# Low weights first, a written-out order, and another address for the values in a two-layer attention trunk

## The chip, the cores and the metric

The kernel runs on one core of a Trainium2 chip. The metric is the device time of one execution in microseconds (us). TensorE (PE) multiplies and adds up in PSUM; ScalarE (ACT), VectorE (DVE) and GpSimd (POOL) do the elementwise work; SyncE (SP) issues the loads. In the profile, PEld is the loading of a product's stationary operand.

## The reference

Two layers, 256 tokens of 1024 channels, everything in float32. A layer normalises its input once, projects it with one matrix of 9808 columns, and splits the result into queries, keys, values and gates of three attention branches (a, b, c) of 8 heads of 64, the small indexer of branch b, the forget logits of branch c and the merge gates:

```python
h = rms_norm(x, gain)
proj = jnp.einsum('bsd,de->bse', h, w_in)
...
y = jnp.einsum('nbsw,nwd->bsnd', jnp.stack([oa, ob, oc], axis=0), w_branch)
gates = jax.nn.sigmoid(merge_logit).reshape(B, S, N_BRANCH, D_MODEL)
merged = jnp.sum(gates * y, axis=2)
return x + jnp.einsum('bsd,de->bse', merged, w_out)
```

Branch a is causal attention, branch b attends to the 64 best keys of its indexer, branch c adds a decay to its logits. Each branch's output is multiplied by its SiLU gate. A final normalisation ends the trunk.

## The kernel before

**Products in halves.** Every float32 operand of a large product is split into a high half, rounded to the matmul's format (tiles `wh`, `hTh`, `og0h`), and a low half, the rest (`wl`, `hTl`, `og0l`). A product is then three: high by high, high weights by the low half of the input, low weights by the high half of the input. ACT makes the high half of a piece of weights (L450), DVE the low half (L454), from a raw tile that SP has loaded; there are six buffers for each half.

**Units.** `unit_b` computes 128 columns of the projection for all 256 tokens: eight steps along the channels, 24 products of 256 columns, cut into four groups of six that the order treats as one operation each (`mm_ops`, L492). Weights are the stationary operand, the normalised input `hTh`/`hTl` moves. `UNIT_ORDER` says how high (nh) and low (nl) products follow each other; the first group holds six high products and no low one. There are 64 such units in a layer: four of the indexer (qi), twelve of each branch (queries q, keys k, gates g, of four pairs of heads), and 24 merge gates (m00 to m27: branch, then block of 128 channels). `unit_y` is the product with the branch matrix, 12 products in two groups; `unit_a` multiplies the other way around, with the input stationary and 512 columns of weights moving, for values (va, vb; L1119 in the first layer, and L1179 in `va_units`) and for the output matrix (o00, o01, o10, o11: half of the columns, then half of the tokens). Units write to one of three PSUM banks (`proj`).

**Attention.** For each pair of heads: scores (`qk`, L713 and L715) into two banks `s`; row minimum and bias on DVE (L781), exponentials on ACT (L785), rounding into a high and a low half (L793 on ACT or L796 on DVE, L800 on DVE), a transpose by DMA for each head (L809, from `e` to `t`), copies of the transposed weights to `pt` (L814 on ACT or L815 on DVE), the product with the values (`av`, L827 to L830) into the one bank `o`. ACT (L843) and DVE (L845) empty that bank into `ot`, L848 applies the gate, and L482/L483 split the result. Evacuations of units: L992 (merge gates, ACT), L1023 and L1025 (branch products, DVE), L742 (gates), L541 to L544 (rotary embedding), L858 to L872 (keys).

**The value tiles.** `V` is two tiles of 8192 bytes per partition. They hold the high and low halves of the values, and are the stationary operand of `av`. At the end of a layer they hold the merged branches and are the stationary operand of the output products (names `proj<-wh,v`). The two tiles stand behind `ncs` and `csum`, 64 bytes each, and begin at 128 modulo 512 bytes.

**The order.** All work after the start is given to a planner as numbered operations (3226 of them, numbered in the order in which the program makes them), each with its engines, its cost, its dependencies, its buffers and a key. The planner walks through modelled time: for each engine it takes, among the operations that can start within `SLACK` of the earliest, the one with the lowest key. `SHIFT` moves keys of single operations by hand, and `WAY` shifts the choice between ACT and DVE (or POOL and DVE) for those that can run on either. The instructions are emitted in that order, so that each engine has a fixed queue; at run time, semaphores alone decide when each starts. PE, ACT, DVE and POOL work their queues strictly in that order, and SP issues weight loads, row loads and transposes in one queue.

**The numbers that the prediction names.** On PE: 1285 is the second `av` of branch b in layer 0, 2578 and 2623 are the two of the second half of branch c in layer 1; 1500 and 1515 are the first groups of the merge gate units m13 and m15 of layer 0. On ACT: 1236 and 1238 empty the bank after the first `av` of branch b, 1270 is the first copy of transposed weights for 1285 and 1284 the last, 1323 writes half of a query tile, 1361 a key tile, 1491 and 1498 are high halves of merge gate weights. On DVE: 1499 is the low half for m13, 3069 and 3076 are those for m14 and m15 of layer 1, 3181 multiplies the first half of the last 128 rows by the final gain. On SP: 1269 and 1282 are the transposes for 1285.

Of the kernel before, what the change touches and what calls it, by code (L numbers as in the profile page):

```python
# [38 lines left out]
STEP = 24.0  # L39
# [5 lines left out]
SLACK = {"PE": 0.0, "ACT": 110.0, "DVE": 110.0, "SP": 1500.0}  # L45
# [12 lines left out]
UNIT_ORDER = ((6, 1), (3, 1), (3, 2), (2, 1), (1, 2), (1, 1))  # L58
# [5 lines left out]
def constants(forget_bias):  # L64
# [26 lines left out]
SHIFT = {  # L91
# [1217 lines left out]
```

## Time and profile before

| | |
|---|---|
| runs | 597.23, 594.69, 596.69 us; median 596.69 |
| profiled execution | 597.11 us, span 595.3 us, granted clock 0.999 |
| TensorE busy | 585.3 us, 98% of the span, 4704 products |
| VectorE, ScalarE, GpSimd busy | 537.7 us, 464.6 us, 94.7 us |
| read from memory | 103.42 MB, 175 GB/s over the span |

A row of groups gives line, engine, operation, output and inputs by the program's names (buffer numbers left out), shapes and count, then busy time in us and mean ns of one, then the engine's idle time just before them and what ended it. A row of the timeline gives start in us, duration in us, and the instruction; equal neighbours are merged (`x2`), and idle time before it stands in brackets. A row of the chain gives start, duration and what the time went to. Products are pipelined: a product's duration reaches into the next ones, so the pace is the distance between starts.

### The profile page before, as it was taken

How to read it: one execution, taken by the hardware profiler on the slowest of the kernel's cores; microseconds unless marked ns; L12 is line 12 of the kernel's file. 1: busy time of each engine (PE TensorE's matmuls, PEld its weight loads, DVE VectorE, ACT ScalarE, POOL GpSimd, SP SyncE). 2: the span in 40 equal slices, each digit the busy share in tenths (PEclk: the TensorE clock that was granted, in tenths of full speed). 3: DMA queues.
4: the chain of work that ended last, by engine and by line, in shares of the span. 5: the costliest groups of instructions: out<-in, count | busy, mean ns of one | idle time of the engine just before them, and what ended most of it. 6: DMA issues, size and time to landing. Idle time of an engine off the chain costs nothing.

```text
span 595.3 us, 12660 instructions
## 1 busy us (share of the span) xinstructions
PE 585.3 (98%) x4704; PEld 566.8 (95%) x4704; DVE 537.7 (90%) x1357; ACT 464.6 (78%) x1006; POOL 94.7 (16%) x103
## 2 busy tenths in 40 slices
PE   8999999999999998999999999999999999999996
PEld 7999999999998998999889999999999989999985
DVE  8879999999899988999685999999999989999883
ACT  6669579997998778975585776899889876999741
POOL 1034041100000224200000510430100004330100
PEclk9999999999999999999999999999999999999999
DMA  8994485798867758296747547697869686655911
GB/s 307 300 300 142 142 264 118 223 219 260 200 188 169 237 179 183 72 267 229 227 142 248 177 143 216 178 225 167 245 184 279 129 222 192 183 141 119 325 36 72
DMA packets 136511, 116.83 MB, mean 196 GB/s; under 512 B 42753, under 2 KB 127361, under 8 KB 136449
## 3 DMA queue, kind: packets, MB, share of 16 engines
q1 hardware_dynamic: 136160, 115.59, 67.5%
q8 instruction: 37, 0.61, 0.4%
q10 hardware_dynamic: 288, 0.43, 0.2%
q14 instruction: 26, 0.20, 0.1%
HBM read 103.42 MB, written 1.05 MB: 175 GB/s over the span
## 4 chain that ended last, share of the span: by engine, by line
PE 89%; DVE 3%; DMA 3%; ACT 3%; issue 1%; POOL 0%; SPq 0%; POOLq 0%; DVEq 0%; ACTq 0%
PE proj L492 75%; PE proj L1179 4%; DMA t<-e 2%; PE s L715 2%; PE proj L1119 2%; PE s L713 2%; PE o L827 1%; PE o L830 1%; DMA raw<-in_x_dram 1%; DVE wl L454 1%; ACT e L785 1%; ACT wh L450 1%; PE o L829 0%; PE o L828 0%; DVE e L800 0%
## 5 line engine op out<-in xcount | busy, mean ns | idle before, releaser
L492 PE MATMUL proj<-hTl,wh 128*128 128x256 f32 x1024 | 264.1, 276 | 0.0
L492 PE MATMUL proj<-hTh,wh 128*128 128x256 f32 x1024 | 263.9, 277 | 0.2 <-DVE mth L1023 0.2
L454 DVE TENSOR_TENSOR wl<-raw,wh 128x1024 fp32r<-128x1024 f32 x180 | 220.4, 1235 | 13.1 <-ACT wh L450 12.0
L492 PE MATMUL proj<-hTh,wl 128*128 128x256 f32 x1024 | 226.2, 277 | 0.0
L450 ACT ACTIVATE wh<-raw 128x1024 fp32r<-128x1024 f32 x180 | 188.3, 1055 | 43.4 <-PE proj L492 34.6
L492 PEld LDWEIGHTS proj<-hTh,wh 128*128 128x128 f32 x1024 | 192.2, 188 | 0.6 <-issue 0.4
L492 PEld LDWEIGHTS proj<-hTl,wh 128*128 128x128 f32 x1024 | 192.2, 188 | 0.1
L492 PEld LDWEIGHTS proj<-hTh,wl 128*128 128x128 f32 x1024 | 172.1, 188 | 0.0
L542 POOL TENSOR_TENSOR rsh<-rsh,cst 128x256 f32<-128x256 f32 x40 | 35.6, 891 | 342.4 <-DVE rsh L541 324.1
L544 POOL TENSOR_TENSOR rr<-rr,rsh 128x256 f32<-128x256 f32 x40 | 44.1, 1103 | 3.1
L785 ACT ACTIVATE e<-e,st 128x128 f32<-128x128 f32 (+1 forms) x96 | 42.6, 445 | 2.0 <-DVE st L781 1.7
L800 DVE SCALAR_TENSOR_TENSOR e<-e,st 128x128 f16<-128x128 f32 (+1 forms) x96 | 39.8, 425 | 0.9 <-ACT e L793 0.4
L814 ACT ACTIVATE pt<-t 128x384 fp32r<-128x384 f16 x73 | 34.3, 514 | 7.4 <-DMA t<-e 6.0
L492 PE MATMUL proj<-wh,v 128*128 128x512 f32 (+1 forms) x144 | 35.2, 366 | 0.0
L492 PE MATMUL proj<-og0l,wh 128*128 128x256 f32 x128 | 33.9, 277 | 0.0
L793 ACT ACTIVATE e<-e,st 128x256 f16<-128x256 f32 (+1 forms) x77 | 32.0, 444 | 0.8 <-DVE e L800 0.2
L492 PE MATMUL proj<-og0h,wh 128*128 128x256 f32 x128 | 32.5, 277 | 0.0
L492 PEld LDWEIGHTS proj<-wh,v 128*128 128x128 f32 x144 | 25.3, 189 | 4.2
L492 PE MATMUL proj<-og0h,wl 128*128 128x256 f32 x128 | 28.8, 278 | 0.0
L492 PEld LDWEIGHTS proj<-og0h,wh 128*128 128x128 f32 x128 | 24.1, 188 | 0.0
L492 PEld LDWEIGHTS proj<-og0l,wh 128*128 128x128 f32 x128 | 24.1, 188 | 0.0
L845 DVE TENSOR_TENSOR ot<-o,ot 64x256 f32<-64x256 f32 x48 | 19.9, 414 | 3.5 <-ACT ot L843 2.7
(225 smaller groups left out, 1072.3 us busy)
## 6 DMA issues: line engine op xcount, KB each, us to landing
raw<-in_w_in_dram SPq DMA_DIRECT2D x74, 1024.0 KB, 5.6
raw<-in_w_branch_dram SPq DMA_DIRECT2D x24, 512.0 KB, 4.1
raw<-in_w_out_dram SPq DMA_DIRECT2D x8, 1024.0 KB, 7.9
raw<-in_x_dram SPq DMA_DIRECT2D x8, 256.0 KB, 5.8
tmp<-wf SPq DMA_DIRECT2D x16, 128.0 KB, 5.5
t<-e SPq DMA_TRANSPOSE x48, 2.9
raw<-in_w_in_dram SPq DMA_DIRECT2D x2, 320.0 KB, 6.9
x<-in_x_dram SPq DMA_DIRECT2D x2, 256.0 KB, 4.5
```

What stands on the lines that cost most here:

```text
L450: ACT.activation(p[0].v, sel(c.v), AF.Copy)
L454: DVE.tensor_tensor(p[1].v, sel(c.v), p[0].v.bitcast(F32), op=ALU.subtract)
L492: PE.matmul(o(), a(), b(), start=first and i == 0, stop=last and i == n - 1)
L542: gps(lambda: POOL.tensor_tensor(T(sh)[:np_], T(sh)[:np_], s[:np_], op=ALU.mult), S, [k_rope], [sh], key, "rope")
L544: gps(lambda: POOL.tensor_tensor(T(r)[:np_], T(r)[:np_], T(sh)[:np_], op=ALU.add), S, [sh], [r], key, "rope")
L713: PE.matmul(o.rearrange("p (h c) -> p h c", h=2), qh[:, sl], kl[:, :, :n], start=True, stop=False)
L785: act(lambda t=t, a=a, n=n, st=st, h=h: ACT.activation(ex(h, a, n), ex(h, a, n), AF.Exp, bias=T(st)[:, t:t + 1], scale=-1.0, accum_out=T(s ...
L793: ACT.activation(hi(a, n), ex(h, a, n), AF.Copy, scale=T(st)[:, 4 + t:5 + t])
L800: dve(lambda t=t, a=a, n=n, st=st, h=h, hi=hi, lo=lo: DVE.scalar_tensor_tensor(lo(a, n), ex(h, a, n), T(st)[:, 4 + t:5 + t], hi(a, n), op0 ...
L814: plan.op([("ACT", t_act(384, False), lambda to=to, src=src: ACT.activation(to(), src(), AF.Copy)), ("DVE", t_dve2(384), lambda to=to, src ...
L845: dve(lambda r=r, h=h: DVE.tensor_tensor(T(t)[r], T(o)[:64, h * S:(h + 1) * S], T(t)[r], op=ALU.add), S, [o], [kt[h]], key, "og", touch=[t ...
L1179: PE.matmul(T(ps[t])[:, :w], hA[hi](a + x, t), T(p[wi])[:, ats[w > 256][wi]][:, :n * w].rearrange("p (k c) -> p k c", k=n)[:, x], start=le ...
```

## The change

Four things. In `unit_b` the 24 products are dealt to the four groups by `UNIT_ORDER` as a list of indices, where 0 to 15 are the high-weight products (each step of the channels by `hTh`, then by `hTl`) and 16 to 23 the low-weight ones. Each group now begins with a low-weight product, has a second one in third place, and ends with high ones. In `unit_y` each of the two groups begins with a low-weight product as well.

The planner no longer chooses: `SHIFT`, `WAY` and `SLACK` are gone, and `ORDER` lists for each engine the operations by number; the walk through modelled time only merges the five lists. The numbers of operations and their contents, other than the order of products within a unit, are the same, since the groups are cut as before. Counted in the lists: PE has 858 operations before and after; 34 operations go to another engine (21 from ACT to DVE, 7 from DVE to ACT, 3 each way between POOL and DVE), so that DVE has 1196 instead of 1182 and ACT 886 instead of 900. The place of an operation on PE moves by up to 19, on SP by up to 8.

`V` is made ahead of `ncs` and `csum`, and so begins at 0 modulo 512 bytes; `ncs` and `csum` follow it, and all tiles behind them keep their addresses.

```diff
@@ -42,7 +42,6 @@
-SLACK = {"PE": 0.0, "ACT": 110.0, "DVE": 110.0, "SP": 1500.0}
...
-UNIT_ORDER = ((6, 1), (3, 1), (3, 2), (2, 1), (1, 2), (1, 1))
+UNIT_ORDER = ((16, 0, 17, 1, 2, 3),
+              (18, 4, 19, 5, 6, 7),
+              (20, 8, 21, 9, 10, 11),
+              (22, 12, 23, 13, 14, 15))
...
-SHIFT = {
-    0: -12, 1: -7.5, 3: -12, 4: -11.5, 25: 4.5, 28: 1, 35: -1, 38: -7.5, 45: -4, 46: -11.5, 47: -4, 71: -12,
...
-WAY = {
-    46: 1500, 99: 1500, 485: 1500, 490: -1500, 498: 1500, 509: 1500, 534: -1500, 535: 1500, 548: -1500, 553: -1500,
...
+ORDER = {
+    "PE": """
...
+1354 1396 1355 1440 1356 1235 1397 1398 1399 1441 1444 1445 1451 1466 1285 1452 1453 1454 1366 1482 1467 1468 1469
+1483 1409 1486 1493 1494 1495 1487 1496 1500 1501 1502 1508 1509 1510 1503 1515 1511 1516 1517 1523 1393 1524 1525
...
+2679 2689 2683 2686 2690 2691 2578 2692 2698 2713 2699 2623 2700 2701 2729 2714 2715 2716 2737 2730 2731 2732 2746
...
+3188 3205 3212 3192 3195 3206 3207 3208 3213 3214 3215""",
+    "ACT": """
...
+1480 1336 1322 1238 1270 1323 1491 1236 1361 1498 1284 1337 1364 1241 1404 1362 1288 1286 1407 1405 1338 1455 1506
...
+3110 3166 3169 3183 3125 3140 3134 3149 3186 3190 3155 3193 3173 3180 3197 3210 3201 3204 3220 3224""",
+    "DVE": """
...
+1471 1372 1411 1373 1385 1423 1484 1375 1424 1410 1376 1499 1414 1488 1507 1388 1415 1427 1389 1514 1428 1418 1419
...
+2938 2986 3069 2950 2980 2951 3076 2989 2990 2981 3084 2992 2991 3091 2993 2994 3099 3020 3022 3023 3114 2997 2996
...
+3211 3217 3181 3216 3218 3221 3222""",
+    "POOL": """
...
+2705 2718 2720 2762 2764 2812 2814 2878 2893 2880 2895 2920 2922 2802 2963 2965 2852 3005 3051 3133 3200 3219""",
+    "SP": """
...
+900 913 1118 1133 1164 1181 1000 1013 1192 1045 1058 1293 1308 1339 1350 1437 1448 1479 1490 1219 1232 1505 1269 1282
...
+2982 2995 3142 3158 3165 3182 3189 3157 3203 3223 3225""",
 }
...
-    def run(self, slack):
+    def run(self, order):
+        lanes = {e: [self.ops[int(n)] for n in s.split()] for e, s in order.items()}
+        free, last, at = {"SP": 1700.0}, {}, dict.fromkeys(lanes, 0)
+        while any(at[e] < len(l) for e, l in lanes.items()):
+            best = None
+            for e, l in lanes.items():
+                if at[e] == len(l) or l[at[e]].need:
+                    continue
+                o, t, short = l[at[e]], free.get(e, 0.0), {}
...
+                if best is None or (t, o.n) < best[:2]:
+                    best = t, o.n, e, o
...
+            t, _, e, o = best
+            w = next(w for w in o.ways if w[0] == e)
+            at[e] += 1
...
     qs = {p: [pool.tile([128, S], F32R, name=f"q{p}{i}") for i in range(3)] for p in "xy"}
+    V = [pool.tile([128, 2, 8, 128], F32R, name=f"v{i}") for i in range(2)]
     ncs = pool.tile([128, 2, 8], F32, name="ncs")
     csum = pool.tile([128, 2, 8], F32, name="csum")
-    V = [pool.tile([128, 2, 8, 128], F32R, name=f"v{i}") for i in range(2)]
     qs.update({p: [pool.tile([128, S], F32R, name=f"q{p}{i}") for i in range(3)] for p in "h"})
...
         his = [(lambda k=k: p[0].v[:, k], lambda k=k, h=h: h[:, k], [p[0]] + hT_all[i])
                for k in range(KC) for i, h in enumerate((hTh, hTl))]
         los = [(lambda k=k: p[1].v[:, k], lambda k=k: hTh[:, k], [p[1]] + hT_all[0]) for k in range(KC)]
-        g, i, j = [], 0, 0
-        for nh, nl in UNIT_ORDER:
-            g += his[i:i + nh] + los[j:j + nl]
-            i, j = i + nh, j + nl
-        n = UNIT_ORDER[0][0]
-        for a, b in ((0, n), (n, 12), (12, 18), (18, 24)):
-            mm_ops(o, g[a:b], t_mm(256), [ps], u, name, a == 0, b == 24)
+        g = his + los
+        for i, part in enumerate(UNIT_ORDER):
+            mm_ops(o, [g[k] for k in part], t_mm(256), [ps], u, name, i == 0, i == 3)
         return u, ps
...
-        g = [g[i] for i in (0, 1, 3, 2, 4, 5, 6, 7, 9, 10, 8, 11)]
+        g = [g[i] for i in (2, 0, 5, 1, 3, 4, 8, 6, 11, 7, 9, 10)]
...
-    PLAN_T[0] = plan.run(SLACK)
+    PLAN_T[0] = plan.run(ORDER)
```

More of the change, by code (lines that the diff above doesn't have):

```diff
@@ L88, in constants @@
     return c
-SHIFT = {
[36 rows of a table removed]
-}
-WAY = {
[6 rows of a table removed]
+ORDER = {
+    "PE": """
[34 rows of a table added]
+3188 3205 3212 3192 3195 3206 3207 3208 3213 3214 3215""",
+    "ACT": """
[35 rows of a table added]
+3110 3166 3169 3183 3125 3140 3134 3149 3186 3190 3155 3193 3173 3180 3197 3210 3201 3204 3220 3224""",
+    "DVE": """
[48 rows of a table added]
+3211 3217 3181 3216 3218 3221 3222""",
+    "POOL": """
[3 rows of a table added]
+2705 2718 2720 2762 2764 2812 2814 2878 2893 2880 2895 2920 2922 2802 2963 2965 2852 3005 3051 3133 3200 3219""",
+    "SP": """
[7 rows of a table added]
+2982 2995 3142 3158 3165 3182 3189 3157 3203 3223 3225""",
 }
@@ L140 @@
 PLAN_T = [0]
-PREV = {}
 class Tok:
@@ L191, in op @@
         o.n, o.out, o.need, o.end = len(self.ops), [], 0, None
-        o.key += SHIFT.get(o.n, 0.0)
-        if len(ways) > 1 and o.n in WAY:
-            o.ways = [w + (WAY[o.n],) if w[0] == "DVE" else w for w in ways]
         for d in o.deps:
@@ L209, in seen @@
         return d.done + (1500.0 if e == "SP" else 200.0 if d.eng == "PE" else 79.0 if e == "POOL" else 33.0)
-    def run(self, slack):
-        free, last = {"SP": 1700.0}, {}
+    def run(self, order):
+        lanes = {e: [self.ops[int(n)] for n in s.split()] for e, s in order.items()}
+        free, last, at = {"SP": 1700.0}, {}, dict.fromkeys(lanes, 0)
         port = {"DVE": 0.0, "POOL": 0.0}
-        ready = [o for o in self.ops if o.need == 0]
-        done = 0
-        while ready:
-            best = {}
-            cand = []
-            for o in ready:
-                t = 0.0
-                short = {}
+        while any(at[e] < len(l) for e, l in lanes.items()):
[4 more added lines that the diff above has]
+                o, t, short = l[at[e]], free.get(e, 0.0), {}
                 for b in o.bufs:
@@ L224, in run @@
                         short[b.tag] = short.get(b.tag, 0) + 1
-                ok = all(b.slot is not None or b.no < self.taken.get(b.tag, 0) + short[b.tag] for b in o.bufs)
-                for g, c in short.items() if ok else ():
-                    f = self.tags[g]
-                    if len(f) < c:
-                        ok = False
-                        break
-                    t = max(t, sorted(x[0] for x in f)[c - 1])
-                if not ok:
-                    continue
-                bw = None
@@ L235, in run @@
-                for w in o.ways:
-                    e = w[0]
-                    tt = max(t, free.get(e, 0.0))
-                    if e in last and (o.half or last[e].half):
-                        tt = max(tt, last[e].done + STEP)
-                    for b in o.bufs:
-                        if b.last is not None and b.last.eng != e:
-                            tt = max(tt, self.seen(b.last, e))
-                    for d in o.deps:
-                        tt = max(tt, self.seen(d, e) + (0.0 if d.eng == e else o.margin) - o.quick)
-                    if e == "POOL" or (e == "DVE" and o.port):
-                        tt = max(tt, port["DVE" if e == "POOL" else "POOL"] - 138.0)
-                    if bw is None or tt + w[1] + sum(w[3:]) < bw[0] + bw[1][1] + sum(bw[1][3:]):
-                        bw = (tt, w)
@@ L249, in run @@
-                cand.append((bw[0], o.key, o.n, o, bw[1]))
-                e = bw[1][0]
-                if e not in best or bw[0] < best[e]:
-                    best[e] = bw[0]
-            if not cand:
-                raise RuntimeError("plan is stuck: " + ", ".join(o.name for o in ready[:20]))
-            e = min(best, key=best.get)
-            lim = best[e] + slack.get(e, 0.0)
-            t, _, _, o, w = min((c for c in cand if c[4][0] == e and c[0] <= lim), key=lambda c: (c[1], c[2]))
@@ L258, in run @@
-            ready.remove(o)
+                if any(b.slot is None and b.no >= self.taken.get(b.tag, 0) + short[b.tag] for b in o.bufs):
+                    continue
+                if any(len(self.tags[g]) < c for g, c in short.items()):
+                    continue
+                for g, c in short.items():
+                    t = max(t, sorted(x[0] for x in self.tags[g])[c - 1])
+                if e in last and (o.half or last[e].half):
+                    t = max(t, last[e].done + STEP)
@@ new lines, in run @@
+                for b in o.bufs:
+                    if b.last is not None and b.last.eng != e:
+                        t = max(t, self.seen(b.last, e))
+                for d in o.deps:
+                    t = max(t, self.seen(d, e) + (0.0 if d.eng == e else o.margin) - o.quick)
+                if e == "POOL" or (e == "DVE" and o.port):
+                    t = max(t, port["DVE" if e == "POOL" else "POOL"] - 138.0)
+                if best is None or (t, o.n) < best[:2]:
+                    best = t, o.n, e, o
@@ L259, in run @@
+            if best is None:
+                raise RuntimeError("order is stuck: " + ", ".join(l[at[e]].name for e, l in lanes.items() if at[e] < len(l)))
+            t, _, e, o = best
+            w = next(w for w in o.ways if w[0] == e)
+            at[e] += 1
             for b in o.bufs:
@@ L264, in run @@
                     self.taken[b.tag] = self.taken.get(b.tag, 0) + 1
-                    PREV.setdefault(o.n, []).extend(b.slot[2] if len(b.slot) > 2 else [])
             o.eng, o.start, o.end = e, t, t + w[1]
@@ L273, in run @@
             w[2]()
-            done += 1
             for b in o.bufs:
@@ L279, in run @@
                 b.end = max(b.end, self.seen(o, "SP" if b.tag == "raw" else "ACT"))
-                b.users = getattr(b, "users", []) + [o.n]
                 if b.left == 0:
-                    self.tags[b.tag].append([b.end, b.slot[1], b.users])
+                    self.tags[b.tag].append([b.end, b.slot[1]])
             for q in o.out:
                 q.need -= 1
-                if q.need == 0:
-                    ready.append(q)
-        assert done == len(self.ops)
         return max(o.done for o in self.ops)
```

160 rows, old and new, of tables (ORDER, SHIFT, WAY) are left out of this document.

## The prediction

> **What bounds the kernel now.** I read the page first: busy time, then the chain that ended last.
>
> ```profile
> PE 585.3 (98%) x4704; PEld 566.8 (95%) x4704; DVE 537.7 (90%) x1357; ACT 464.6 (78%) x1006; POOL 94.7 (16%) x103
> PE 89%; DVE 3%; DMA 3%; ACT 3%; issue 1%; POOL 0%; SPq 0%; POOLq 0%; DVEq 0%; ACTq 0%
> L492 PE MATMUL proj<-hTh,wh 128*128 128x256 f32 x1024 | 263.9, 277 | 0.2 <-DVE mth L1023 0.2
> L454 DVE TENSOR_TENSOR wl<-raw,wh 128x1024 fp32r<-128x1024 f32 x180 | 220.4, 1235 | 13.1 <-ACT wh L450 12.0
> ```
>
> TensorE is the bound, and almost nothing on it waits. A product's 277 ns is the time from its start to its end, and the next starts long before that; what counts is the distance between starts. The chain in order of time gives it where PE runs without a break:
>
> ```profile
> 59.32 15.08 PE proj L492 x132
> 89.69 15.64 PE proj L492 x138
> 149.52 15.67 PE proj L492 x138
> 358.49 19.78 PE proj L492 x174
> 485.34 22.47 PE proj L492 x198
> ```
>
> 88.64 us for 780 products is 113.6 ns each; the best of these pieces has 113.3. The change removes no product, so some 570 us of PE work stay, and only four things can move: waits of PE, the small excess over 113.3 ns, the products that read the value tiles, and the two ends. The profiled execution took 597.11 us (span 595.3); the median of the runs is 596.69, 0.42 lower, and I take that off at the end. About 0.5%, 3 us, is what a measurement of this kernel can tell from no change.
>
> **Waits of PE and the new lists.** I went through the timeline of PE for starts that lie further apart than the work between them. After the first 13 us three places stand out. The largest, PE first, then ACT, DVE and the chain:
>
> ```profile
> 235.81 0.39 PE L492 MATMUL proj<-og1h,wl 128*128 128x256 f32 x2
> 237.93 0.39 PE L827 MATMUL o<-pt,v 128*128 128x256 f32 x1 [1.73 <-DVE ot L845]
> 234.15 0.94 ACT L814 ACTIVATE pt<-t 128x384 fp32r<-128x384 f16 x2 [1.64 <-DMA t<-e]
> 235.09 0.42 ACT L699 ACTIVATE qx<-qy 64x256 fp32r<-64x256 f32 x1
> 235.52 0.38 ACT L843 ACTIVATE ot<-o 64x256 f32<-64x256 f32 x1
> 237.90 1.04 ACT L450 ACTIVATE wh<-raw 128x1024 fp32r<-128x1024 f32 x1
> 237.47 0.41 DVE L845 TENSOR_TENSOR ot<-o,ot 64x256 f32<-64x256 f32 x1
> 227.77 6.29 DMA t<-e
> ```
>
> The last of two products started at 235.92, the next should at 236.04, and started at 237.93: 1.9 us lost. There is one bank for o, and the step before had to be emptied of it. ACT copies it out (235.52), but in ACT's queue that copy stood behind two copies of transposed weights, whose transposes took 6.29 us to land. In the new ACT list the first of the two emptying copies (1238) stands ahead of the late one (1270); the second (1236) still stands behind it, behind a q copy (1323) and a wh half (1491). By the rows that is 234.15 + 0.47 (half of 0.94) + 0.42 + 1.04 + 0.38 on ACT and 0.41 on DVE: the bank is free at 236.9. The step itself (1285) stands two groups of six later on PE, 2 x 6 x 0.1133 = 1.36 us, and arrives at 237.4. But its own last copy (1284) now stands behind a bd copy and another wh half, until about 238.3. So some 0.9 of 1.9 stays and 1.0 goes (bounds 0 and 1.9).
>
> ```profile
> 479.27 0.28 PE L830 MATMUL o<-pt,v 128*64 128x256 f32 x1
> 479.92 0.39 PE L827 MATMUL o<-pt,v 128*128 128x256 f32 x1 [0.37 <-ACT pt L814]
> 483.71 0.28 PE L492 MATMUL proj<-hTl,wh 128*128 128x256 f32 x1
> 484.39 0.36 PE L827 MATMUL o<-pt,v 128*128 128x256 f32 x1 [0.40 <-DVE ot L845]
> 207.23 0.28 PE L492 MATMUL proj<-hTl,wh 128*128 128x256 f32 x1
> 207.70 0.35 PE L492 MATMUL proj<-hTh,wh 128*128 128x256 f32 x1 [0.20 <-DVE mth L1023]
> ```
>
> Against 0.11 us these lose 0.54, 0.57 and 0.36. Steps 2578 and 2623 stand one and two groups later in the new list (0.68 and 1.36 us), and their scores two and one earlier; the lists around 207 change little. I take 1.2 of these 1.5 us (bounds 0 and 1.5). Together with the short restart after each wait (about 0.1 us each, four of them) the waits give 2.6 us; what would be late next is the low half of the weights.
>
> **Low weights first.** A unit's first group now needs its low half, which DVE makes with the 1.235 us instruction above; before, six high products came first. That costs nothing where the low half lies ready by more than those 0.68 us; I matched the 152 low halves of units with 256-wide products with the starts of the units' first groups: in five the group started before the half was done. The first and the second of the five, DVE's instruction and PE's start, and a row for what follows:
>
> ```profile
> 249.95 1.21 DVE L454 TENSOR_TENSOR wl<-raw,wh 128x1024 fp32r<-128x1024 f32 x1
> 248.58 0.28 PE L492 MATMUL proj<-hTh,wh 128*128 128x256 f32 x1
> 254.82 1.21 DVE L454 TENSOR_TENSOR wl<-raw,wh 128x1024 fp32r<-128x1024 f32 x1
> 254.77 0.28 PE L492 MATMUL proj<-hTh,wh 128*128 128x256 f32 x1
> L815 DVE CAST pt<-t 128x384 fp32r<-128x384 f16 x23 | 8.5, 386 | 2.0 <-DMA t<-e 1.9
> ```
>
> The first started 251.16 - 248.58 = 2.6 us too early. In the new PE list that group (1500) stands four places later, 4 x 0.68 = 2.7 us, which covers it; in DVE's list the low half (1499) stands three places later, and 3 x 0.4 us (DVE's 537.7 us over its 1357 instructions) is open again. The second was short by 256.03 - 254.77 = 1.3 us, and its group (1515) stands two places later, 1.36 us; the other three lacked less. PE is in order: while it waits here, every group behind it waits, and with them the evacuations on ACT and DVE. In layer 1's twin of this stage the low halves of m14 and m15 (3069, 3076) stand 8 and 10 places later on DVE. DVE also receives work: its list has 14 operations more, mostly copies and roundings of attention weights, at most 14 x 0.386 = 5.4 us, beside 13.1 us of idle time ahead of the low halves alone. Between 0 and 3 us of new waits (the worst shortage and a little more); I take 0.9, near the 1.2 left open in the worst place.
>
> The other side of the same edit is the pace. After attention steps the products run slow for a while:
>
> ```profile
> 247.88 0.28 PE L492 MATMUL proj<-hTh,wh 128*128 128x256 f32 x1
> 249.76 0.40 PE L492 MATMUL proj<-og1h,wl 128*128 128x256 f32 x2
> 250.58 0.28 PE L492 MATMUL proj<-hTl,wh 128*128 128x256 f32 x1
> 252.51 0.28 PE L492 MATMUL proj<-hTh,wl 128*128 128x256 f32 x1
> ```
>
> 16 products, all with high weights, from 247.88 to 249.76 are 117.5 ns each; the 17 from 250.58, with low weights among them, 113.5. Summed over all starts of 256-wide products at L492, such stretches hold 2.4 us, and the first group of a unit, the six high ones, has more of it per product than any later one. Some end with a low product, some only after several. I take half, 1.2 us (bounds 0 and 2.4).
>
> **The value tiles.** V was read as the loaded operand in the last units and in attention's second product:
>
> ```profile
> 583.73 0.64 PE L492 MATMUL proj<-wh,v 128*128 128x256 f32 x4
> 588.76 0.64 PE L492 MATMUL proj<-wh,v 128*128 128x256 f32 x4
> 238.40 0.28 PE L827 MATMUL o<-pt,v 128*128 128x256 f32 x1
> 238.75 0.28 PE L492 MATMUL proj<-hTh,wh 128*128 128x256 f32 x1
> ```
>
> From 583.73 to 588.76 lie 42 products, 119.8 ns each against 113.3 with other weights: 48 x 6.5 ns = 0.31 us. From 238.40 to 238.75 lie 768 columns, 340 ns at the usual pace: 10 to 14 ns too many in each of 48 heads, 0.5 to 0.7 us. If the offset is the cause the gain is up to 0.9 us; if the moving operand is, nothing. I take 0.6.
>
> The Trainium skill, in "TensorE: Matmul & The Clock Gate", section "Step-by-step: what each phase is for", speaks against both of these gains: it says that TensorE has two separate read ports into SBUF, and that loading the next weights takes no read bandwidth from the running product. By that rule neither the offset nor which half is loaded first changes the pace. The rows above, with a pace that differs by the operands, do not agree with it outright.
>
> **The ends.** At the start the lists swap a few steps of the first values; the load of constants moves behind the next weights on SP's queue, where no early product reads them. PE's idle time there is short:
>
> ```profile
> 7.25 0.33 PE L615 MATMUL s<-cst,tmp 128*128 128x128 f32 x1 [0.53 <-DVE tmp L601]
> 588.57 0.15 DVE L651 SCALAR_TENSOR_TENSOR fsum<-fsum 128x1 f32<-128x1 f32 x1
> 589.68 0.42 DVE L1270 TENSOR_TENSOR x<-x,proj 128x256 f32<-128x256 f32 x1 [0.96 <-PE proj L492]
> 580.03 0.69 DVE L646 TENSOR_TENSOR x<-x,acc 128x512 f32<-128x512 f32 x1 [0.85 <-ACT acc L644]
> ```
>
> I set it at nothing, 0.5 either way. At the end one multiplication (3181, 0.69 us, now at 580.03) moves into DVE's gap of 0.96 before the last residual, while the work ahead of that gap moves one group later (0.7): the gap covers a part, and about 0.2 us is added (0 to 0.4).
>
> **The sum.** -2.6 (waits) + 0.9 (new waits) - 1.2 (pace) - 0.6 (values) + 0.2 (end) = -3.3: the profiled execution at 593.8, the median at 593.4, -0.55%.
>
> **The rivals.** *The pace follows neither the weights nor the address*, but the moving operand and the attention steps that go before: the waits change as above, the 1.8 us of both gains stay away, 595.2. For it: the slow stretches follow attention steps, and several contain low products. Against it: 119.8 and 113.3 in the rows. It is what the section of the Trainium skill named above would have. *The waits come back*: SP's list around the late transposes is the same in both kernels, so they will again land 6 us after their issue behind a load of weights, and an in-order ACT stands still again. Then the 2.6 us stay and only the pace gains against the new waits' 0.9 plus the end's 0.2: 596.69 - 1.8 + 1.1 = 596.0. *Slower, by low halves that come late*: PE waits for DVE at the head of unit after unit in the stage of the merge gates, at 245 to 260 and 535 to 550. The five shortages, if nothing covers them, are 2.6 + 1.3 + 0.8 + 0.7 + 0.4 = 5.8 us; m14 and m15 of layer 1, 8 to 10 places at 0.4 us, about 3 more. That replaces my 0.9: 593.4 + 7.9 = 601.3. It decides from some 7 us of waits for wl. Against it: the PE list puts the five groups later by about what they lack.
>
> **How the numbers follow.** Forecast 0.50; pace unmoved 0.22; waits back 0.19; late low halves 0.09. The two middle ones end within 3 us: faster 0.50, same 0.41, slower 0.09. With every gain at its bound and nothing added (1.9 + 1.5 + 0.4 of waits, 2.4, 0.9: 7.1) the time is 589.6. Upwards the range takes in both middle rivals, the later one with 1.2 us more of new waits: 597.2. Outside lie the slower case and the far ends of the others.
>
> **What would show it.** Right: in the timeline of PE no gap at the step behind 236 larger than 1 us and none at 479 and 484; 16 products after an attention step nearer 113.5 than 117.5; the last units at 113 to 114 ns; PE's waits for wl, all together, near 1 us. Wrong: PE rows that wait for DVE wl L454 at heads of units, or the last units still at 119.8. Nothing of it holds if PE's total of products or the granted clock differs.

## The result and the profile after

The change makes the kernel slower: median 600.07 us (six runs, 599.28 to 600.97) against 596.03 us of before on the same chip (six runs, 594.69 to 597.23). The ratio is 1.0067, with a 95% interval from 1.005 to 1.0084. The profiled execution of after took 599.69 us with a span of 597.9, that of before 597.11 with 595.3. The profiles thus differ by 2.6 us and the medians by 4.0: the profiled execution of before lies 1.1 above its median, that of after 0.4 below its own. The working below explains the 2.6.

Line numbers have moved by 68 to 72 places: L564 is the products' line (L492 before), L526 the low halves (L454), L522 the high halves (L450), L895 to L898 the product with the values (L827 to L830), L911 and L913 the emptying of its bank (L843, L845). The page of after, busy time, the chain that ended last, and two groups:

```profile
PE 590.0 (99%) x4704; PEld 568.9 (95%) x4704; DVE 539.3 (90%) x1371; ACT 462.2 (77%) x992; POOL 88.4 (15%) x103
PE 84%; DVE 6%; DMA 5%; ACT 4%; issue 1%; SPq 0%; ACTq 0%
L564 PE MATMUL proj<-hTh,wl 128*128 128x256 f32 x1024 | 260.5, 279 | 0.5 <-ACT mth L1060 0.3
L526 DVE TENSOR_TENSOR wl<-raw,wh 128x1024 fp32r<-128x1024 f32 x180 | 220.2, 1235 | 8.7 <-ACT wh L522 8.2
```

The products are the same 4704, and PE is *busier* by 4.7 us. A product's time reaches until its end, so a product that starts late or runs at a slower pace fills more of the span; more busy time is not more work. The chain is the telling line: DVE, DMA and ACT now stand on the path for 15% of the span, before for 9%. The idle time ahead of the low halves fell, 13.1 to 8.7 us; whether PE waited for them is read from its own waits below.

Where the long waits were, the timeline of PE in after has none:

```profile
239.33 0.28 PE L564 MATMUL proj<-hTl,wh 128*128 128x256 f32 x1
239.44 0.28 PE L895 MATMUL o<-pt,v 128*128 128x256 f32 x1
...
482.99 0.61 PE L564 MATMUL proj<-wl,hTh 128*128 128x512 f32 x2
483.44 0.28 PE L895 MATMUL o<-pt,v 128*128 128x256 f32 x1
...
487.47 0.28 PE L564 MATMUL proj<-hTl,wh 128*128 128x256 f32 x1
487.58 0.28 PE L895 MATMUL o<-pt,v 128*128 128x256 f32 x1
```

The step that stood still at 236 follows its neighbour by 0.11 us, and so does the second of the two that stood still at 479 and 484; the first follows two products of 512 columns after 0.45 us, just their pace. What came instead are short ones at the heads of groups. PE and then ACT at the longest of them, then PE and DVE at the second:

```profile
416.58 0.28 PE L564 MATMUL proj<-hTl,wh 128*128 128x256 f32 x1
417.11 0.38 PE L564 MATMUL proj<-hTh,wl 128*128 128x256 f32 x1 [0.25 <-ACT mth L1060]
417.33 0.28 PE L564 MATMUL proj<-hTh,wh 128*128 128x256 f32 x1
...
416.26 0.53 ACT L882 ACTIVATE pt<-t 128x384 fp32r<-128x384 f16 x1 [0.84 <-DMA t<-e]
416.69 0.37 ACT L1060 ACTIVATE mth<-proj 128x256 f32<-128x256 f32 x1
```

```profile
161.47 0.28 PE L564 MATMUL proj<-og0l,wh 128*128 128x256 f32 x1
161.93 0.39 PE L564 MATMUL proj<-hTh,wl 128*128 128x256 f32 x1 [0.19 <-DVE acc L1086]
...
160.32 1.23 DVE L526 TENSOR_TENSOR wl<-raw,wh 128x1024 fp32r<-128x1024 f32 x1
161.47 0.41 DVE L1086 SCALAR_TENSOR_TENSOR acc<-acc,proj 128x256 f32<-128x256 f32 x1
```

Both are the same thing: a new unit needs a PSUM bank, and the evacuation of that bank starts late, because in its engine's queue it stands behind a copy of transposed weights (416.26), or behind a low half (160.32). The first gap is 0.53 us from start to start instead of 0.11. The next product then starts 0.22 us later, another 0.11 lost at the restart. PEld's waits, by what ended them, name the banks too (columns: us in total, times, longest):

```profile
PEld proj L564 <- DVE g L810: 0.6, 3, 0.3
PEld proj L564 <- ACT mth L1060: 0.4, 1, 0.4
PEld proj L564 <- DVE acc L1086: 0.4, 1, 0.4
```

For the whole span I took the distance from each start to the next and subtracted 0.4427 ns for each column, the pace of the undisturbed pieces (113.3 ns for 256). The rest is counted as a gap if it is over 60 ns, and as slow pace if not:

| us | before | after | difference |
|---|---|---|---|
| gaps over 0.3 us, from 17 to 583 us | 3.35 (4 gaps) | 0.77 (2) | -2.58 |
| shorter gaps, there | 2.31 (24) | 5.65 (54) | +3.34 |
| gaps at the start | 6.47 | 6.63 | +0.15 |
| slow pace, output products with the values | 0.37 | 1.38 | +1.01 |
| slow pace, the rest | 8.55 | 9.07 | +0.52 |
| from the last product's start to the end | 5.95 | 6.09 | +0.14 |
| sum | | | +2.6 |

In this pair of profiles the long gaps went, and short ones gave back more. Sorted by what the late weight load waited for, with the restart behind it, evacuations of banks hold 3.13 us of after's gaps from 17 to 583 us and 0.44 of before's, waits inside attention 0.93 and 3.29, and the rest 2.35 and 1.92.

A profile is one execution, so other ones matter here. Runs 1, 6, 9 and 10 below have the lists and the order of products of before, runs 2, 4 and 5 the lists of after. The five profiles with before's lists have 22 to 24 short gaps (2.1 to 2.3 us) and 2.2 to 4.1 us of long ones, together 4.3 to 6.4 us. The four with the new lists have 49 to 54 short gaps (4.7 to 5.8 us) and 0.3 to 1.4 us of long ones, together 5.0 to 6.7 us. The exchange of long gaps for short ones is thus in every profile, but the surplus of 0.8 us in this pair is less than what the total varies by. Of before's four long waits, those at 207 and 236 us stand in all five profiles, the one at 484 in two, and the one at 479 in this one alone.

The other large item is the values. Groups with their shapes kept apart, of before and then of after:

```profile
L492 PE MATMUL proj<-wh,v 128*128 128x512 f32 x112 | 30.1, 390 | 0.0
L492 PE MATMUL proj<-wl,v 128*128 128x512 f32 x56 | 17.3, 389 | 0.0
```

```profile
L564 PE MATMUL proj<-wh,v 128*128 128x512 f32 x112 | 30.8, 396 | 0.0
L564 PE MATMUL proj<-wl,v 128*128 128x512 f32 x56 | 17.6, 395 | 0.0
```

All 168 products of 512 columns take 6 ns longer, 1.0 us. The first of these groups is the gauge for the address in all that follows.

### The profile page after: what moved, and what is told of

Read it like the earlier page. It is cut to its first block, busy times and chain, and to the rows that moved or that the text cites. A ratio compares the mean times of both kernels' runs of the same rounds, so it can differ in the third digit from the quotient of the medians.

```text
span 597.9 us, 12660 instructions
## 1 busy us (share of the span) xinstructions
PE 590.0 (99%) x4704; PEld 568.9 (95%) x4704; DVE 539.3 (90%) x1371; ACT 462.2 (77%) x992; POOL 88.4 (15%) x103
## 4 chain that ended last, share of the span: by engine, by line
PE 84%; DVE 6%; DMA 5%; ACT 4%; issue 1%; SPq 0%; ACTq 0%
PE proj L564 70%; PE proj L1247 4%; DMA t<-e 3%; PE proj L1187 2%; PE s L781 2%; PE s L783 2%; DVE wl L526 2%; ACT wh L522 1%; DMA raw<-in_w_in_dram 1%; PE o L898 1%; DMA x<-in_x_dram 1%; PE o L895 1%; ACT e L853 1%; DVE e L868 0%; PE o L897 0%
## 5 line engine op out<-in xcount | busy, mean ns | idle before, releaser
L564 PE MATMUL proj<-hTh,wh 128*128 128x256 f32 x1024 | 283.4, 277 | 0.0
L564 PE MATMUL proj<-hTh,wl 128*128 128x256 f32 x1024 | 260.5, 279 | 0.5 <-ACT mth L1060 0.3
L564 PE MATMUL proj<-hTl,wh 128*128 128x256 f32 x1024 | 258.4, 277 | 0.0
L526 DVE TENSOR_TENSOR wl<-raw,wh 128x1024 fp32r<-128x1024 f32 x180 | 220.2, 1235 | 8.7 <-ACT wh L522 8.2
L522 ACT ACTIVATE wh<-raw 128x1024 fp32r<-128x1024 f32 x180 | 187.9, 1054 | 28.3 <-PE proj L564 14.4
L564 PEld LDWEIGHTS proj<-hTh,wl 128*128 128x128 f32 x1024 | 192.2, 188 | 1.8 <-ACT mth L1060 0.4
L564 PEld LDWEIGHTS proj<-hTh,wh 128*128 128x128 f32 x1024 | 192.2, 188 | 0.1
L564 PEld LDWEIGHTS proj<-hTl,wh 128*128 128x128 f32 x1024 | 192.3, 188 | 0.0
L612 POOL TENSOR_TENSOR rr<-rr,rsh 128x256 f32<-128x256 f32 x40 | 38.3, 961 | 5.5 <-DVE rr L611 2.8
L564 PE MATMUL proj<-wh,v 128*128 128x512 f32 (+1 forms) x144 | 35.9, 370 | 0.0
L564 PE MATMUL proj<-og0h,wh 128*128 128x256 f32 x128 | 35.5, 277 | 0.0
L861 ACT ACTIVATE e<-e,st 128x256 f16<-128x256 f32 (+1 forms) x68 | 29.6, 451 | 5.3 <-DVE e L868 2.9
L564 PE MATMUL proj<-og0h,wl 128*128 128x256 f32 x128 | 33.0, 282 | 0.1
L564 PE MATMUL proj<-og0l,wh 128*128 128x256 f32 x128 | 32.4, 277 | 0.0
L564 PEld LDWEIGHTS proj<-wh,v 128*128 128x128 f32 x144 | 25.2, 188 | 4.9
L913 DVE TENSOR_TENSOR ot<-o,ot 64x256 f32<-64x256 f32 x48 | 20.0, 416 | 5.5 <-ACT ot L911 4.3
L911 ACT ACTIVATE ot<-o 64x256 f32<-64x256 f32 x48 | 18.2, 378 | 8.3 <-PE o L898 7.3
L564 PEld LDWEIGHTS proj<-og0h,wl 128*128 128x128 f32 x128 | 24.0, 188 | 0.5 <-DVE g L810 0.4
```

The lines of the kernel that those rows point to most:

```text
L522: ACT.activation(p[0].v, sel(c.v), AF.Copy)
L526: DVE.tensor_tensor(p[1].v, sel(c.v), p[0].v.bitcast(F32), op=ALU.subtract)
L564: PE.matmul(o(), a(), b(), start=first and i == 0, stop=last and i == n - 1)
L612: gps(lambda: POOL.tensor_tensor(T(r)[:np_], T(r)[:np_], T(sh)[:np_], op=ALU.add), S, [sh], [r], key, "rope")
L861: ACT.activation(hi(a, n), ex(h, a, n), AF.Copy, scale=T(st)[:, 4 + t:5 + t])
L911: act(lambda r=r, h=h: ACT.activation(T(t)[r], T(o)[64:, h * S:(h + 1) * S], AF.Copy), S, True, [o], [kt[h]], key, "og", touch=[t], half=True)
```

## Experiments

**Theories.** A: the address costs time, because weights of the output product (the moving operand) begin at 128 modulo 512 bytes and the values (the loaded one) now begin at 0; what counts is the distance. B: the lists remove the long waits and pay for them in short ones. Rivals: the address is harmless and the loss lies in the lists alone; the low products at heads of units cost the time, either by waits for `wl` or by pace. The first four runs share one chip and one median of before, 596.54 us, the next four another, 596.94, the last three 596.70. Ratios are to before, with 95% intervals. "Low first" stands for the new `UNIT_ORDER` and the new order in `unit_y`.

**1. The address alone**, in before:

```diff
+    V = [pool.tile([128, 2, 8, 128], F32R, name=f"v{i}") for i in range(2)]
     ncs = pool.tile([128, 2, 8], F32, name="ncs")
     csum = pool.tile([128, 2, 8], F32, name="csum")
-    V = [pool.tile([128, 2, 8, 128], F32R, name=f"v{i}") for i in range(2)]
```

> The kernel before with nothing changed but the place of the two value tiles (0 instead of 128 modulo 512 bytes). Address theory: the 144 output products that load the values against high weights, and the 72 against low weights, go from 226.6 to about 233 ns at 512 columns, as in the profile of the changed kernel, so about 1.1 us more than before (597.1 for 596.0), with no new wait. Port theory (address without effect): same as before within 0.3 us, the 512-wide output products at 227 ns. My prediction's term: 0.6 us less.

597.81 us, 1.0019 (1.0007 to 1.0032): slower by 1.1 to 1.3 us. Its row:

```profile
L492 PE MATMUL proj<-wh,v 128*128 128x512 f32 x112 | 30.8, 396 | 0.0
```

The same 396 ns as in after. The address is a loss by itself.

**2. The lists alone**: after, with the old order of products in `unit_b` and `unit_y`, and the values at 128.

```diff
-UNIT_ORDER = ((16, 0, 17, 1, 2, 3),
-              (18, 4, 19, 5, 6, 7),
-              (20, 8, 21, 9, 10, 11),
-              (22, 12, 23, 13, 14, 15))
+UNIT_ORDER = ((0, 1, 2, 3, 4, 5),
+              (16, 6, 7, 8, 17, 9),
+              (10, 11, 18, 19, 12, 13),
+              (20, 14, 21, 22, 15, 23))
...
-        g = [g[i] for i in (2, 0, 5, 1, 3, 4, 8, 6, 11, 7, 9, 10)]
+        g = [g[i] for i in (0, 1, 3, 2, 4, 5, 6, 7, 9, 10, 8, 11)]
```

> The five written-out lists of the changed kernel, with the old order of products in a unit and the values at the old address. If the parts add up (lists good, low weights first and the address bad): the waits at 236 and 479 stay away and few come in their place, 1 to 2 us less than before (594 to 595). If the lists themselves are what costs: still 1.5 us or more above before (597.5 or more), with PE's new waits in 17 to 74, 240 to 300 and 380 to 460 still there.

599.0 us, 1.0043 (1.0027 to 1.0058). The lists alone lose 2.5 us. PEld's waits in this run:

```profile
PEld proj L564 <- DVE rr L611: 1.3, 2, 1.1
PEld proj L564 <- DVE g L810: 0.6, 2, 0.4
```

Banks again, and no low half, since the units' first groups are all high here. In the count between 17 and 583 us it has 52 gaps with 6.74 us (before 28 with 5.65), and its slow pace is 0.65 us above before. The short waits come from the lists, not from the order within a unit.

**3. Low first alone**: the new order of products with the lists of before, written out, and the values at 128.

```diff
@@ before, with the planner's lists written out as ORDER
+UNIT_ORDER = ((16, 0, 17, 1, 2, 3),
+              (18, 4, 19, 5, 6, 7),
+              (20, 8, 21, 9, 10, 11),
+              (22, 12, 23, 13, 14, 15))
...
-        g = [g[i] for i in (0, 1, 3, 2, 4, 5, 6, 7, 9, 10, 8, 11)]
+        g = [g[i] for i in (2, 0, 5, 1, 3, 4, 8, 6, 11, 7, 9, 10)]
```

> The order of the kernel before, written out as lists, with the values at the old address, and only the products within a unit in the new order (low weights first). If low weights first is what costs: 2 to 4 us above before (598 to 600), with waits of PE for wl at heads of units around 70, 250 and 256 (2.6, 1.3, 0.8 us short) and a restart of 0.11 instead of 0.08 us after each wait. If it costs only through the lists it was given: within 1 us of before. My prediction's pace term alone: 1.2 us less.

600.91 us, 1.0077 (1.0055 to 1.0098), the worst of all. PE's waits, PE's timeline and DVE's at the longest of them, and the windows around it (us, busy time of PE, PEld, DVE, ACT, POOL, granted clock, share of the DMA engines, GB/s):

```profile
PE proj L564 <- DVE wl L526: 3.0, 3, 2.4
```

```profile
249.07 0.28 PE L564 MATMUL proj<-hTl,wh 128*128 128x256 f32 x1
251.77 0.58 PE L564 MATMUL proj<-hTh,wl 128*128 128x256 f32 x1 [2.42 <-DVE wl L526]
252.15 0.41 PE L564 MATMUL proj<-hTh,wh 128*128 128x256 f32 x1
252.36 0.41 PE L564 MATMUL proj<-hTh,wl 128*128 128x256 f32 x1
...
250.51 1.20 DVE L526 TENSOR_TENSOR wl<-raw,wh 128x1024 fp32r<-128x1024 f32 x1
```

```profile
249.00:251.70 2.70, 0.34 (x4) 0.14 (x2) 2.64 (x12) 2.18 (x8) 0.46 (x1) 0.94 0.36 51
251.70:254.50 2.80, 2.73 (x13) 2.73 (x14) 0.09 (x2) 0.00 (x0) 0.00 (x0) 0.50 0.71 193
```

At 249.07 PE stands for 2.59 us (2.70 from start to start, less 0.11), until the low half is done. That is the place and nearly the size that the prediction read from the trace of before (a group 2.6 us too early there). It costs a second time: the clock falls to half, and a dozen products start 0.21 us apart. Its slow pace is 0.45 us *below* before's, but without the output products the five profiles with before's lists and order range over 0.35 us, and this one lies only 0.1 under the lowest: a gain in pace isn't shown. The order within a unit does a lot of harm where the lists don't have the low halves ready in time. After's lists do: there no PE row waits for `wl` at L564.

**4. After without the address**: after, with the values behind `ncs` and `csum` again.

```diff
-    V = [pool.tile([128, 2, 8, 128], F32R, name=f"v{i}") for i in range(2)]
     ncs = pool.tile([128, 2, 8], F32, name="ncs")
     csum = pool.tile([128, 2, 8], F32, name="csum")
+    V = [pool.tile([128, 2, 8, 128], F32R, name=f"v{i}") for i in range(2)]
```

> The changed kernel with only the values put back to 128 modulo 512 bytes. Address theory: about 1.1 us less than the changed kernel (599.0 for 600.1), the 512-wide output products back at 227 ns. Port theory: no difference from the changed kernel (600.1).

598.43 us, 1.0031 (1.0017 to 1.0045). From run 2 to this one is low first with the new lists: 0.6 us by the medians, inside the intervals; in the profiles slow pace falls by 0.54 us and gaps by 0.82, 0.25 of it at the start. Profiles with the same lists and the same order differ by about as much. From this one to after is the address: 1.0031 to 1.0067, 2.1 us by the two ratios, which come from different chips, and 1.4 us by slow pace in the two profiles, 0.9 of it in the output products.

**5 and 6. The distance.** The table `MOVING` says where the weights of a product begin modulo 512 bytes; its entry O belongs to the output product. It is moved in after and in before:

```diff
-MOVING = {"V": (192, 192), "C": (128, 0), "CK": (384, 384), "O": (128, 128)}
+MOVING = {"V": (192, 192), "C": (128, 0), "CK": (384, 384), "O": (0, 0)}
```

> The changed kernel with the moving weights of the output product shifted to 0 instead of 128 modulo 512 bytes, so that they again begin at the same offset as the values that are loaded. If the distance between the two offsets sets the pace: the 512-wide output products are back at 227 ns, and the time is near that of the changed kernel with the values put back (598.4). If the values' own address sets it: 233 ns as in the changed kernel (600.1).

> The kernel before with only the moving weights of the output product shifted to 0 modulo 512 bytes, the values left at 128. If the distance between the offsets sets the pace: 232 to 234 ns and about 1.1 us more than before (597.6). If only the values' address counts: as before (596.5).

After with O at 0: 598.64 us, 1.0036 (1.002 to 1.0051). Before with O at 0: 596.81, 1.0008 (0.9994 to 1.0023). Their rows, after's and then before's:

```profile
L564 PE MATMUL proj<-wh,v 128*128 128x512 f32 x112 | 30.2, 391 | 0.0
```

```profile
L492 PE MATMUL proj<-wh,v 128*128 128x512 f32 x112 | 30.6, 395 | 0.0
```

With both operands at 0 after has the pace of before; with weights at 0 and values at 128 before has the pace of after. Neither address is good or bad in itself: the distance between the two decides. In before the loss of 0.9 us that the starts show stays inside the interval of the time.

**7. Low first where it has time**: the lists of before, values at 128, a first group that is all high, and low ones first from the second group on; `unit_y` begins low as in run 3.

```diff
+UNIT_ORDER = ((0, 1, 2, 3, 4, 5),
+              (16, 6, 17, 7, 18, 8),
+              (19, 9, 20, 10, 21, 11),
+              (22, 12, 23, 13, 14, 15))
```

> The order of before and the old addresses; in a unit, only the second, third and fourth group begin with a low-weight product (in first, third and fifth place), and the first group stays six high products. If low weights first cost by the wait for them at the head of a unit: no waits for wl above 0.3 us, and the 4.4 us that the new order of products cost with these lists are gone (596 to 597). If it costs by the products' own order (pace, restarts): still 598 or more. The small excess of pace should be 0.2 to 0.5 us lower than before.

596.51 us, 1.0000 (0.9986 to 1.0014). The loss of run 3 is gone with the low products at the heads of `unit_b`'s units, and the long wait at 236 is there as in before. Slow pace was 9.8 us against 8.9, with 0.5 of the difference in the first 5 us: no gain in pace shows, and the time is that of before.

**8. The long waits alone**: the lists of before with six operations at other places. On ACT, the two copies that empty the bank (1238, 1236) stand ahead of the late copy 1270; on DVE 1237 behind 1239; on PE the three steps that stood still, 1285, 2578 and 2623, stand behind 1451, 2691 and 2700. The places on ACT, DVE and PE:

```diff
-1491 1270 1271 1337 1238 1322 1323 1236 1284
+1491 1238 1236 1270 1271 1337 1322 1323 1284
...
-1465 1239 1400 1283 1402 1237 1442
+1465 1239 1237 1400 1283 1402 1442
...
-1444 1445 1285 1451 1452
+1444 1445 1451 1285 1452
...
-2689 2690 2578 2691 2692 2698 2623 2699 2700 2701
+2689 2690 2691 2578 2692 2698 2699 2700 2623 2701
```

> The kernel before with its own lists and four moves: ACT's two copies that empty the bank o ahead of the late copies of transposed weights at 234, DVE's second addition right behind its first, and the three attention steps that waited (236, 479, 484) one to two groups later on PE. If those waits cost what their gaps say: 1.2 to 2.6 us less than before (594 to 595.3), the gap at 236 under 0.7 us, and those at 479 and 484 gone. If the waits only move: as before within 0.5 us (596 to 597).

595.41 us, 0.9982 (0.9963 to 1.0001). The gaps from 200 to 240 us fall from 2.44 to 0.11 us, those from 460 to 486 from 1.29 to nothing. The wait at 207, 0.44 us of the first sum with its restart, is missing too, though no move touches it. Yet this profile's span is 595.3, as before's. PE's waits:

```profile
PE proj L564 <- DVE mth L1091: 1.6, 1, 1.6
PE proj L564 <- DVE g L810: 0.7, 1, 0.7
```

These are two waits for banks, at 269 and at 497 us. The first is not the price of the moves: runs 1, 9 and 10, with before's lists untouched, have it too, with 0.8 to 1.0 us, while before and run 6 don't. In run 9, PE's waits and ACT's row just ahead:

```profile
PE proj L492 <- DVE mth L1023: 1.0, 2, 0.8
269.16 2.01 ACT L450 ACTIVATE wh<-raw 128x1024 fp32r<-128x1024 f32 x2 [1.27 <-DMA raw<-in_w_out_dram]
```

ACT stood still until a load of output weights had landed, and on DVE the low half and then the evacuation came late with it. In before ACT started the same two roundings at 267.44 without a wait. So the same lists wait there in one execution and not in the next, by when a load lands. The median fell by 1.5 us, but the interval reaches 1.0001: a small gain, not quite clear of none.

**9 and 10. Other distances**, one execution each: before, with O at 64 (64 bytes from the values) and at 384 (256 bytes).

```diff
-MOVING = {"V": (192, 192), "C": (128, 0), "CK": (384, 384), "O": (128, 128)}
+MOVING = {"V": (192, 192), "C": (128, 0), "CK": (384, 384), "O": (64, 64)}
...
+MOVING = {"V": (192, 192), "C": (128, 0), "CK": (384, 384), "O": (384, 384)}
```

> Before, with the output weights starting at 64 instead of 128 modulo 512 bytes (values at 128: 64 bytes apart). The excess over 0.4427 ns a column in the 112 products wh,v of 512 columns was 0.05 us with no distance and 0.62 to 0.73 us at 128 bytes. If any distance costs the same: 0.6 to 0.75 us. If it grows with the distance: near 0.35 us. If 64 bytes are still within one access: near 0.05 us. The time itself moves by less than one run can tell.

> Before, with the output weights starting at 384 instead of 128 modulo 512 bytes (values at 128: 256 bytes apart). If any distance costs the same: 0.6 to 0.75 us of excess in the 112 products wh,v of 512 columns. If it grows with the distance: near 1.3 us. If only an odd multiple of 128 bytes costs something: near 0.05 us. The time itself moves by less than one run can tell.

598.05 and 597.28 us, one run each, of which nothing follows. The rows, 64 bytes and then 256:

```profile
L492 PE MATMUL proj<-wh,v 128*128 128x512 f32 x112 | 30.7, 396 | 0.0
```

```profile
L492 PE MATMUL proj<-wh,v 128*128 128x512 f32 x112 | 30.1, 390 | 0.0
```

At 64 bytes the excess of the 112 products was 0.72 us, at 256 it was 0.06. A distance of 64 or 128 bytes costs the same 5 to 6 ns a product, 0 or 256 none. It doesn't grow with the distance: of the expectations, "any distance costs the same" fails at 256, "it grows" at both, and "near 0.05 us" at 64.

**11. The best of the parts**: run 8's places and run 7's `UNIT_ORDER` together, in the lists of before with the values at 128. `unit_y` has the order of before here, unlike in run 7.

```diff
-1444 1445 1285 1451 1452
+1444 1445 1451 1285 1452
...
+UNIT_ORDER = ((0, 1, 2, 3, 4, 5),
+              (16, 6, 17, 7, 18, 8),
+              (19, 9, 20, 10, 21, 11),
+              (22, 12, 23, 13, 14, 15))
```

> The lists of before with the four moves of the run that mended the waits at 236, 479 and 484, and with the unit order whose first group is all high and whose groups 2 to 4 begin low; the values stay at 128. If the two edits add up (0.9982 and 1.0000 of before): 1.1 us under before, with no gap over 0.3 us between 200 and 240 us and none between 460 and 486. If the mended waits only move about, as the profile of the first of them hints (2.4 us of new gaps between 240 and 300), the time is within 0.5 us of before and the excess in big gaps stays near 12 us. If the low halves come late once more work runs just in time, PE waits for DVE wl appear and it is 1 us or more over before.

596.04 us against 596.70, 0.9982 (0.9967 to 0.9996), with 594.9 us for the profiled execution (span 593.0): a small gain over before, 0.7 us by the medians and 1.1 by the ratio, and by the two ratios (0.9982 and 1.0067 of 596 us) 5.1 us less than after. PE's waits behind the start are one row, and PE goes through 236 without a gap:

```profile
PE proj L564 <- DVE mth L1091: 0.2, 1, 0.2
```

```profile
236.87 0.28 PE L564 MATMUL proj<-hTl,wh 128*128 128x256 f32 x1
236.98 0.28 PE L895 MATMUL o<-pt,v 128*128 128x256 f32 x1
237.10 0.22 PE L896 MATMUL o<-pt,v 128*128 128x128 f32 x1
```

It has 25 gaps with 2.80 us between 17 and 583 us, against 28 with 5.65 in before. The waits of run 8 at 269 and 497 are not in this profile. The first comes and goes with before's own lists (run 8), so its absence is no merit of the order of products; a long wait at 497 is in no other profile. The ratios of the two runs are equal, so that the order adds nothing that these runs show.

## Why the prediction was wrong

Forecast was a gain of 3.3 us on the profiled execution; it lost 2.6. By the prediction's own terms:

**The waits (-2.6) is the step that failed first.** The part on the three places had the direction right, and more went than forecast: the gaps over 0.3 us lost 2.58 us, and the step behind 236 kept none of its forecast 0.9. Some of this is luck. The waits at 479 and 484, 1.1 of the 1.5 us that the prediction counted beside 236, came from one execution; of the five profiles with before's lists, one has the first and two have the second. What failed is the sentence "what would be late next is the low half of the weights". Late next were the evacuations of the PSUM banks: the gaps that they ended, with the restarts, are 3.13 us in after against 0.44 in before. All short gaps together are 30 more, +3.34 us; with 0.15 at the start the waits, old and new, came out at +0.9 instead of -1.7. I had followed the three places that stood out and the operations next to them, and had not gone through the heads of groups in the new lists asking when the bank of each comes free. Run 2 shows the short waits with the lists alone, 3.76 us of them behind evacuations.

**The new waits for low halves (+0.9)** didn't come: none over 0.15 us at L564. The judgement behind it, that the new PE list puts the five groups later by about what they lack, held. Run 3 shows what it would have been without that, 4.4 us; so the rival of late low halves had its mechanism and its place right, but it isn't what made after slower. That the forecast's slower case (601.3) lies near the measured 600.07 is chance.

**The pace (-1.2)** failed. I had read 117.5 against 113.5 ns as a matter of high and low weights. In after, 16 products from just behind the attention step, six of them with low weights:

```profile
240.15 0.28 PE L564 MATMUL proj<-hTh,wl 128*128 128x256 f32 x1
...
241.91 0.28 PE L564 MATMUL proj<-hTl,wh 128*128 128x256 f32 x1
```

1.76 us over 15 distances are 117.3 ns. Low weights don't end the slow stretch. With the new lists low first is worth 0.54 us of slow pace at most (runs 2 and 4), with the old ones 0.45 (run 3), both about the size by which executions of the same lists and order differ (0.35 to 0.5). The lists alone cost 0.65 (run 2); without the output products the four profiles with new lists have 8.6 to 9.2 us of slow pace, the five with before's 8.2 to 8.6. What is slow behind attention steps, and why the lists add to it, stays open.

**The values (-0.6)** had the wrong sign: +1.0 (run 1). The step was "if the offset is the cause", with only a gain or nothing as its ends. The 119.8 ns of the last units was compared with units that have other operands, so it said nothing of the address. In after these units have:

```profile
587.67 0.63 PE L564 MATMUL proj<-wh,v 128*128 128x256 f32 x4
...
591.22 0.64 PE L564 MATMUL proj<-wh,v 128*128 128x256 f32 x4
```

30 products in 3.55 us, 118.3 ns: 1.5 ns a product better, under 0.1 us in all, while the 168 products of 512 columns, which the prediction did not look at, lost 6 each. The attention products kept their pace (mean 222 ns before, 221 after for the second of the four). The Trainium skill's section that the prediction set against these gains ("TensorE: Matmul & The Clock Gate", "Step-by-step: what each phase is for") says that loading weights takes no read bandwidth from the running product. What the prediction concluded from it, no gain from the address, was nearer than my term; but 390 against 396 ns, by the distance of two operands alone (runs 1, 5, 6, 9, 10), does not agree with it outright either.

**The end (+0.2)** was right: 0.14.

```profile
591.81 0.28 PE L564 MATMUL proj<-wl,v 128*128 128x256 f32 x1
...
591.49 0.68 DVE L714 TENSOR_TENSOR x<-x,acc 128x512 f32<-128x512 f32 x1
592.13 0.42 DVE L1338 TENSOR_TENSOR x<-x,proj 128x256 f32<-128x256 f32 x1
```

As forecast, the multiplication (591.49) stands just ahead of the last residual. The residual starts 5.8 us before the end of the span; before it was 5.6 (595.3 less 589.68).

Three things stay open. The profiles account for 2.6 us, and the medians differ by 4.0; the rest is spread between executions that one profile each can't show. The lists cost 1.8 to 2.6 us by the ratios of runs 2, 4 and 5, while the four profiles with them exceed the five with before's lists by only 0.4 us of gaps, 0.6 of slow pace and 0.1 at the end, on average; so the short waits are shown, but not that they are the whole of the lists' loss. And the reason why the evacuations come later in the new lists is read from the rows at 161 and 417, not tried one by one.

## What to carry to other kernels

When a fixed order is exchanged for one that removes the long waits of the busiest engine, go through every head of a group and ask when its PSUM bank comes free in the new queues: thirty more gaps of about 0.1 us, the restarts among them, weighed as much here as the one of 1.9 us and its neighbours. A wait that one profile shows may belong to that execution; look for it in a second one before its removal is counted as a gain. An operand's address had no value of its own here; look at where it begins relative to the operand that it meets, and gauge it by the mean time of just those products, kept apart by shape. A gain that rests on comparing two kinds of products with different operands needs a row in which only the claimed cause differs; where there is none, its lower end is below nothing.

## What the runs showed of the hardware

- The output product of 512 columns takes 5 to 6 ns longer (395 or 396 ns for 390) when the loaded and the moving operand begin 128 bytes apart modulo 512, in either direction (after, runs 1 and 6), or 64 bytes apart (run 9); at 0 (before, run 5) and at 256 bytes (run 10) it doesn't. With 256 columns the same products show the reverse, 283 against 281 ns.
- Behind a gap of 2.6 us on PE the granted clock was half for the next 2.8 us (run 3, 0.50, one execution), about 1.3 us more lost: 13 products at 0.21 instead of 0.11 us. The gaps at 236 of 1.9 us in before and of 2.2 us in run 10 left it at full (1.00).
- After a wait at the head of a group the second product starts 0.22 us behind the first, not 0.11 (161.93 and 417.11 in after): each such wait costs 0.11 us beyond its own length.
